# Log-sum-exp over rows: which block of rows each SBUF partition holds

## The chip, the cores and the metric

The kernel runs on one core of a Trainium2 chip. The metric is the device time of one execution in microseconds; lower is better. "The time" of a kernel is the median of several runs. A profile is one further execution, recorded by the hardware profiler, and it has a time of its own.

## The reference

The input x is 32 x 512 x 1024 in float32, 64 MiB, drawn from a normal distribution. The output is one number per row of 1024, 32 x 512 in float32.

```python
def reference(x, axis):                      # axis = -1
    x_max = np.max(x, axis=axis, keepdims=True)
    return (x_max.squeeze(axis)
            + np.log(np.sum(np.exp(x - x_max), axis=axis))).astype(np.float32)
```

The kernel computes log(sum(exp(x))) without taking the maximum away first; for values of this size that is the same number.

## The kernel before, in words

The input is seen as N = 16,384 rows of D = 1024 numbers (4 KB). P = 128 partitions share them evenly: NB = 128 rows to a partition. Rows are independent of each other, so any partition may hold any block of 128 rows, as long as the result is stored to where the rows came from. Before the change, partition p holds the rows from 128p to 128p+127, a run of 512 KB in HBM (`x_v`, and `out_v` for the result).

The work goes along the 128 rows of every partition in the 17 chunks of `CHUNKS`. A chunk is (rows, rows whose sum DVE takes, parts into which those are cut, whether DVE adds by halves). It starts with 4 rows, then 15, 16, 16, 16, 14, 13, 9, 7, 5, 4, 3, 2, and ends with four of one row. A chunk of r rows is one DMA of 128 x r x 4 KB; its source is one contiguous run of r x 4 KB for each partition, and its destination r slots of `ring`, a buffer of 51 slots of 4 KB per partition.

- Loads: `load` (L97 issues the DMA) runs on SP's queue, in the order of the chunks. Ahead of it SP waits until DVE (and ACT, L96) have used the slots that the chunk is to overwrite. The first load is moved by hand to the front of the program (`n_early`).
- Exponential: ACT waits for a chunk's semaphore (`landed[i]`) and overwrites it in place with exp, for DVE's rows in `parts` pieces (L134), then row by row for the rest, where ACT sums along the way (L161).
- Sums: DVE waits for each piece of ACT's and sums its rows into `sums`, in one instruction (L154), or for the chunks marked so row by row, adding the two halves of a row (L141).
- Logarithm: `take_logs` (L105) runs on ACT three times: over the first chunks at chunk `LN_AT`, over the following ones in the last chunk, and over the last four rows at the very end.
- Store: one DMA on ACT's queue (L173) writes `res`, 128 numbers per partition, 64 KB in all.

The order on each engine is the order in which the loop over the chunks writes its instructions; nothing is reordered by a planner. The change touches the source pattern in `load` and the target pattern of the store.

The softmax here doesn't subtract the row's maximum and nothing guards it: scores larger than these inputs give would overflow.

## Time and profile before

| | |
|---|---|
| time, median of 3 runs | 163.15 us (163.01 to 163.37) |
| the profiled execution's own time | 163.28 us |
| its span, first to last instruction | 161.4 us |
| DVE busy | 121.0 us (75%) |
| ACT busy | 115.1 us (71%) |
| read from HBM | 67.11 MB |
| SP's queue (loads) | 2448 packets |
| ACT's queue (store) | 144 packets |

How to read the profile: the span is cut into 40 equal slices, and a digit is the busy share of a slice in tenths; for DMA it is the mean over the core's 16 DMA engines. The list of DMA queues gives packets, MB, and the time in packets as a share of 16 engines' span. 2448 packets are 17 loads of 128 data packets, one per partition, and 16 that count up the semaphore, one per engine. The chain follows the work that ended last back to what released it at each step. A line of waits is: engine and line, what ended the wait, us in total, times, longest. A line of the stretches is: the stretch and its length, then for each engine busy us and instructions, the TensorE clock, the DMA's mean busy share (where packets reach over a border it can come out a little over 1) and GB/s. The trace also keeps a record of every DMA packet: its start, its duration and its bytes, without an address or an engine's number.

### The profile page before, as it was taken

What the parts mean: (1) busy time and instruction counts of PE and PEld (TensorE: products, weight loads), DVE (VectorE), ACT (ScalarE), POOL (GpSimd) and SP (SyncE); (2) the same over time, 40 slices, a digit from 0 to 9 for tenths busy, and PEclk for the clock granted to TensorE, in tenths of its full rate; (3) what the DMA queues carried; (4) which work ended last, traced back from release to release, by engine and by line L of the source; (5) the groups of instructions that cost most, each with busy time, mean ns of one, the idle gap of its engine ahead of it and who ended that gap; (6) DMA issues with size and microseconds to landing.
All of it is one profiled execution on the core that took longest, in us unless ns stands there. A gap on an engine that the chain in (4) does not pass through costs nothing.

```text
span 161.4 us, 149 instructions
## 1 busy us (share of the span) xinstructions
DVE 121.0 (75%) x46; ACT 115.1 (71%) x40; POOL 0.2 (0%) x4
## 2 busy tenths in 40 slices
DVE  0028000003999999999999699999999999999892
ACT  3170005996079960999519993999199999999995
POOL 0000000000000000000000000000000000000000
DMA  6999699989989989989979999999999999999990
GB/s 256 508 487 457 289 472 520 406 374 520 422 357 520 406 374 520 406 374 520 406 341 455 455 455 439 422 422 422 430 429 429 418 426 415 427 430 417 403 394 24
DMA packets 2592, 67.18 MB, mean 416 GB/s; under 512 B 288, under 2 KB 416, under 8 KB 928
## 3 DMA queue, kind: packets, MB, share of 16 engines
q1 hardware_dynamic: 2448, 67.11, 96.9%
q10 hardware_dynamic: 144, 0.07, 0.1%
HBM read 67.11 MB, written 0.07 MB: 416 GB/s over the span
## 4 chain that ended last, share of the span: by engine, by line
DMA 49%; DVE 29%; ACT 20%; issue 0%
DMA ring<-in_x_dram 49%; DVE sums L154 29%; ACT ring L134 17%; ACT ring L161 3%; ACT res L105 0%
## 5 line engine op out<-in xcount | busy, mean ns | idle before, releaser
L154 DVE TENSOR_REDUCE sums<-ring 128x8 f32<-128x8192 f32 (+5 forms) x14 | 111.2, 7995 | 37.3 <-ACT ring L134 37.2
L134 ACT ACTIVATE ring<-ring 128x8192 f32<-128x8192 f32 (+6 forms) x18 | 104.4, 5835 | 43.9 <-DMA ring<-in_x_dram 43.8
L141 DVE CUSTOM_DVE_ANT_0 ring<-ring 128x512 f32<-128x512 f32 x16 | 9.9, 688 | 0.0
L161 ACT ACTIVATE ring<-ring 128x1024 f32<-128x1024 f32 x9 | 9.3, 1041 | 0.0
L119 ACT ACT_TABLE_LOAD x1 | 1.3, 1283 | 0.8 <-PEq L215 0.8
L161 ACT ACTIVATION_READ_ACCUMULATOR ring<-ring 128x1 f32 x9 | 1.5, 172 | 0.0
L141 DVE DVE_READ_ACCUMULATOR2_ANT sums<- 128x1 f32 x16 | 1.3, 84 | 0.0
L105 ACT ACTIVATE res<-sums 128x81 f32<-128x81 f32 (+1 forms) x2 | 0.5, 246 | 0.0
L105 ACT ACTIVATE res<-late 128x4 f32<-128x4 f32 x1 | 0.2, 173 | 0.0
L215 POOL MEMSET const-bfloat16-1.0<- 128x1 bf16 x1 | 0.1, 103 | 0.0
L215 POOL MEMSET const-uint8-127<- 128x1 uint8 x1 | 0.1, 102 | 0.0
L215 POOL MEMSET const-float32-0.0<- 128x1 f32 x1 | 0.1, 100 | 0.2 <-issue 0.2
L215 POOL MEMSET const-float32-1.0<- 128x1 f32 x1 | 0.1, 99 | 0.0
## 6 DMA issues: line engine op xcount, KB each, us to landing
ring<-in_x_dram SPq DMA_DIRECT2D x1, 7680.0 KB, 25.2
ring<-in_x_dram SPq DMA_DIRECT2D x1, 7168.0 KB, 28.6
ring<-in_x_dram SPq DMA_DIRECT2D x1, 6656.0 KB, 35.7
ring<-in_x_dram SPq DMA_DIRECT2D x1, 4608.0 KB, 20.2
ring<-in_x_dram SPq DMA_DIRECT2D x2, 2048.0 KB, 16.1
ring<-in_x_dram SPq DMA_DIRECT2D x1, 3584.0 KB, 28.3
ring<-in_x_dram SPq DMA_DIRECT2D x1, 2560.0 KB, 27.3
ring<-in_x_dram SPq DMA_DIRECT2D x4, 512.0 KB, 27.0
```

The lines of the kernel that those rows point to most:

```text
L105: nc.scalar.activation(out=res[:, lo:hi], in_=src, func=Ln).then_inc(act_done, 1)
L119: nc.scalar.preload_act_table_set("natural_log_exp_and_others")
L134: nc.scalar.activation(out=ring[:, s + lo : s + hi], in_=ring[:, s + lo : s + hi], func=Exp).then_inc(act_done, 1)
L141: nc.vector.tensor_tensor_reduce(out=ring[:, s + j, : D // 2], in0=ring[:, s + j, : D // 2], in1=ring[:, s + j, D // 2 :], scale=1.0, scal ...
L154: nc.vector.reduce_sum(out=sums[:, row + lo : row + hi], in_=ring[:, s + lo : s + hi], axis=AX).then_inc(dve_done, 1)
L161: nc.scalar.activation(out=ring[:, s + j], in_=ring[:, s + j], func=Exp, accum_out=total(row + j),).then_inc(act_done, 1)
L215: nc = _bacc.Bacc("TRN2", target_bir_lowering=False, num_devices=1)
```

## The change

Partition p no longer holds block p of 128 rows but block p//8 + 16*(p%8): partitions 0 to 7 hold blocks 0, 16, 32, ... 112, partitions 8 to 15 blocks 1, 17, ... 113, and so on. The words that came with the change say that the 16 DMA engines then read blocks next to each other (0.5 MB apart), and that each engine's next block is 8 MB further. A helper `blocks` builds the pattern for both ends: for x with rows of D numbers and a start at row `lo`, for the output with rows of one number. In HBM a pattern has now three levels, 16 blocks at a step of 512 KB, 8 groups of them at a step of 8 MB, and the contiguous run; the SBUF side of the DMAs is as before. Nothing else changes: chunks, waits, instructions and their order are the same.

```diff
-    x_v = x_flat.rearrange("(p t) d -> p t d", p=P)
-    out_v = bass.AP(tensor=out.tensor, offset=out.offset, ap=[[NB, P], [1, NB]])
+    PER, ENG = 8, 16
+    assert P == PER * ENG
+
+    def blocks(ap, width, lo, n):
+        return bass.AP(
+            tensor=ap.tensor,
+            offset=ap.offset + lo * width,
+            ap=[[NB * width, ENG], [ENG * NB * width, PER], [1, n * width]],
+        )
...
-        nc.sync.dma_start(out=ring[:, s : s + r], in_=x_v[:, row : row + r]).then_inc(
+        nc.sync.dma_start(
+            out=ring[:, s : s + r],
+            in_=blocks(x_flat, D, row, r),
+        ).then_inc(
             landed[i], 16
         )
...
-    nc.scalar.dma_start(out=out_v, in_=res).then_inc(stored, 16)
+    nc.scalar.dma_start(
+        out=blocks(out, 1, 0, NB), in_=res
+    ).then_inc(stored, 16)
```

## The prediction

> **What bounds the kernel now.** I read the views from the whole to the part: the slices of the span, the DMA queues, the chain that ended last, the waits (engines, then SP's queue), and the stretches between stage borders.

> The slices and the queues first:

> ```profile
> span 161.4 us, 149 instructions
> ...
> DMA  6999699989989989989979999999999999999990
> ...
> q1 hardware_dynamic: 2448, 67.11, 96.9%
> q10 hardware_dynamic: 144, 0.07, 0.1%
> HBM read 67.11 MB, written 0.07 MB: 416 GB/s over the span
> ```

> The queue that carries the 17 loads has its 16 engines in packets for 96.9% of the span, 156.4 us of 161.4 us. The store's queue is 0.1%.

> The chain and the waits:

> ```profile
> DMA 49%; DVE 29%; ACT 20%; issue 0%
> ...
> ACT ring L134 <- DMA ring<-in_x_dram: 43.8, 7, 14.9
> DVE sums L154 <- ACT ring L134: 37.2, 4, 23.5
> ...
> SPq L97 <- DVE sums L154: 122.9, 7, 52.8
> ```

> The chain gives DVE and ACT half, which could mislead: a step on it is whatever released the next, and a load in flight behind another is not seen. ACT waits for nothing but loads (43.8 us), DVE only for ACT. SP's 122.9 us of waiting for free ring slots does no harm as long as the queue holds a load behind the running one. The queue's share, and this view in order of time, say it does:

> ```profile
> core 0: us, DVE busy (x) ACT busy (x) POOL busy (x), PEclk, DMA share, GB/s
> 0.00:8.00 8.00, 0.00 (x0) 1.80 (x2) 0.20 (x4) 1.00 0.95 385
> 8.00:40.00 32.00, 5.39 (x2) 16.10 (x2) 0.00 (x0) 1.00 1.02 442
> ...
> 117.00:146.00 29.00, 28.91 (x11) 29.00 (x11) 0.00 (x0) 1.00 0.99 426
> 146.00:158.00 12.00, 11.03 (x26) 11.88 (x13) 0.00 (x0) 1.00 0.94 386
> 158.00:161.40 3.40, 0.22 (x2) 1.73 (x6) 0.00 (x0) 1.00 0.07 19
> ```

> The DMA column is at 0.94 to 1.02 up to 158 us. From 117 us DVE (28.91 of 29) and ACT (29.00 of 29) are full too: the tail is packed, and all three end together. So a DMA that is uniformly slower moves the end by its whole delay, and a faster one moves the end by what it has gained up to about 84 us, where DVE waits last for a load through ACT (idle 1.59 us ahead of 91.15).

> How near is the DMA to its ceiling? The trace's packet records (start, duration, bytes; one packet per partition and load) give medians of 611 ns for 16,384 B and 2420 ns for 65,536 B. The slope, 1809 ns for 49,152 B, is 27.2 GB/s per engine and 435 GB/s for 16; what is left, some 9 ns, is a packet's fixed cost. Each engine has 156.21 us of data packets; at the median of each size it would be 155.49 us. The excess is 0.72 us per engine: 0.40 us in the first packet of twelve engines (762 to 1608 ns where the other four took 608 to 612), 0.14 us in fifteen long packets before 45 us, and 0.18 us in many of a few ns each.

> [...] The trace has no addresses; [...] the first packets start in two bunches, seven from 1.01 to 1.31 us and nine from 1.62 to 2.21. [...]

> **The change part by part.**

> *Load source patterns (17 DMAs).* Block p is still 128 rows of 4 KB, 512 KB, but partition p gets block p//8 + 16*(p%8). Bytes, contiguous runs (128 per load, 4 to 64 KB), waits and issue order do not change, so the 2448 packets stay and their time at the medians stays: 155.5 us per engine. Cost 0 in this term [...]; both bounds are below, as rivals.

> *The first packets and the scattered excess.* 0.72 us per engine can go if they come from streams that collide in HBM. [...] But twelve first packets end together with the four that started late (all ends lie between 2.19 and 2.87 us), which looks like one common first-access delay that any order has. I take 0, ends -0.72 and +0.4 (the other four slow as well).

> *Building the descriptors.* The source has one dimension more. SP takes 327 to 779 ns per issue (median 365), the engines' first packets spread over 1.2 us. Only the first load's issue is on the path; each later one has a load before it still in flight, and the cover is thinnest for small loads, whose median from issue to landing is 27.0 us for 1.3 us of own packets. Without that cover each would cost its 0.37 us. If the extra dimension doubled the first issue's 0.37 us, the end moves by 0.4; it can't gain, since 128 runs are still made. I take 0, ends 0 and +0.4.

> *The store.* It is last on ACT, 1.6 us from issue to landing, all on the path. It still has 128 runs of 512 B, of 27 ns each, 8 per engine: 0.22 us. Neighbouring partitions' runs lay side by side in 4 KB and now lie 8 KB apart. If each took twice as long: +0.22; the issue (0.373 us) doubled: +0.37. I take 0, ends -0.1 and +0.6. Nothing is queued behind it but the clearing of semaphores.

> *Compute.* Every ACT and DVE instruction keeps shape and count; rows are independent. 0. No wait is added, so nothing new stands behind one.

> Sum against the profiled execution's own time, 163.28 us (span 161.4, 1.88 around it): 0 + 0 + 0 + 0 = 163.28. That execution is 0.13 above the median of the runs, 163.15, so the forecast for a median is 163.15, say 163.1. From the ends above, the case's own range is 162.8 to 163.5. The measurement can tell about 0.2% (0.33 us) from no change.

> **The rivals.**

> *Faster: collisions in HBM go.* For: the excess hits several engines at once (four 64 KB packets near 44 us took 71 to 329 ns too long). Against: it is 0.5% at most. All of it gone gives 163.15 - 0.72 = 162.43; 0.54 of the 0.72 us lies before 45 us, so the packed tail passes it on. This includes half of it, 162.8.

> *Slower: HBM likes the new spacing less.* [...] It decides once the mean 64 KB packet is 5 ns longer (0.2%).

> *Much slower: the port match breaks.* [...] with 1.0 us ahead of the first packet, 3.4 us after the last and 1.9 around the span, 314 us. [...] 64 KB packets of 4840 ns instead of 2420, and the loads outlast every other engine at once.

> [...]

> **How the numbers follow.** Forecast (no change) 0.40; faster 0.19; slower by HBM, issue or store 0.22; much slower 0.19. Slower together 0.41. The range leaves out the port case alone (0.19) and runs from the low end of the faster case, 162.2 (0.72 us and a little of the uneven end, where engines finish between 156.9 and 158.0), to the high end of the HBM case, 168.6. The likeliest case's own range is 162.8 to 163.5.

> **What would show it.** Right: 64 KB packets stay at 2420 ns, the queue's time at 97% of the span, first packets again up to 1600 ns, ACT's wait for loads at 43.8 us, 1.6 us for the store. Faster: first packets near 611 and a queue share of 156.2 down to 155.6 us. HBM: longer packets of all sizes, evenly, and DVE's gap ahead of 91 us growing. Ports: packets doubled and DVE's share of the span near 40%. The forecast is wrong if packets change length at all, or the spread of the first starts leaves 1.2 us.

## The result, and the profile after

The changed kernel takes 327.96 us (327.31 to 329.44, 6 runs) beside 163.19 us for the kernel before (6 runs as well): 2.011 times as long, 95% interval 2.006 to 2.015. The forecast of no change is wrong, and the time lies outside its range. It is the rival named "the port match breaks", which had 314 us and a chance of 0.19; its signs came too, packets of twice the length and DVE busy for 37% of the span. "Port" is its word for a place where the writes of two engines would meet; no trace shows such a place. The profiled execution has 328.28 us, of which 326.4 are its span.

The page of the changed kernel, the lines that stand for the slices and the queues:

```profile
span 326.4 us, 149 instructions
...
DMA  8959979969989699696998799999999899999994
...
q1 hardware_dynamic: 2448, 67.11, 98.5%
q10 hardware_dynamic: 144, 0.07, 0.1%
HBM read 67.11 MB, written 0.07 MB: 206 GB/s over the span
```

The same 2448 packets and 67.11 MB, and a queue that is as busy as before (98.5% where it was 96.9%), but at half the rate. A busy DMA row therefore says that packets are in flight, not how fast their bytes flow. What changed is the duration of a packet.

Its waits, engines and SP (engine, line, what for: us in total, times, longest):

```profile
ACT ring L146 <- DMA ring<-in_x_dram: 203.7, 13, 34.3
DVE sums L166 <- ACT ring L146: 175.7, 9, 42.9
...
SPq L106 <- DVE sums L166: 243.8, 7, 76.6
```

ACT's wait for loads has gone from 43.8 to 203.7 us; DVE waits for ACT as before. SP's wait has doubled too, but it is no cause, since the queue stays full. The chain of this kernel names half of its length "another core or an unknown queue":

```profile
another core or an unknown queue 50%; ACT 32%; DMA 15%; issue 2%
```

In order of time those pieces lie between one chunk's exponentials and the next (27.48 us after the second chunk, for example), where ACT waits for the load in flight; it is the loads' share under another name.

One stretch in mid-flight (stretch and length, busy us and instructions of DVE, ACT and POOL, TensorE clock, the DMA's share, GB/s):

```profile
50.00:90.00 40.00, 16.15 (x1) 13.00 (x1) 0.00 (x0) 1.00 1.00 206
```

SP's issues of the loads (how many: min/median/max ns, first and last start):

```profile
L106 SPq DMA_DIRECT2D ring<-in_x_dram x17: 536/541/619, 0.0 to 254.0; - x17
```

The list of DMA issues has the store (KB, us to landing):

```profile
out_dram<-res ACTq DMA_DIRECT2D x1, 64.0 KB, 2.1
```

206 GB/s with the engines 100% in packets: by the packet records a 64 KB packet has a median of 5109 ns where it had 2420, and one of 16 KB 1260 where it had 611. An issue takes 541 ns at the median (365 before) and the store 2.1 us to landing (1.6 before).

The span adds up: 1.40 us to the first packet, 320.8 us from there to the end of the last load (156.9 before), 4.2 us after it, and 1.88 us around the span give 328.28.

### The profile page after: what moved, and what is told of

It is laid out like the page before. It is cut to its first block, busy times and chain, and to the rows that moved or that the text cites. A ratio compares the mean times of both kernels' runs of the same rounds, so it can differ in the third digit from the quotient of the medians.

```text
span 326.4 us, 149 instructions
## 1 busy us (share of the span) xinstructions
DVE 121.7 (37%) x46; ACT 116.0 (36%) x40; POOL 0.2 (0%) x4
## 3 DMA queue, kind: packets, MB, share of 16 engines
q1 hardware_dynamic: 2448, 67.11, 98.5%
HBM read 67.11 MB, written 0.07 MB: 206 GB/s over the span
## 4 chain that ended last, share of the span: by engine, by line
another core or an unknown queue 50%; ACT 32%; DMA 15%; issue 2%
ACT ring L146 29%; DMA ring<-in_x_dram 15%; ACT ring L173 2%; ACT res L117 0%
## 5 line engine op out<-in xcount | busy, mean ns | idle before, releaser
L146 ACT ACTIVATE ring<-ring 128x8192 f32<-128x8192 f32 (+6 forms) x18 | 104.6, 5839 | 203.7 <-DMA ring<-in_x_dram 203.7
```

The costliest lines, as they stand in the source:

```text
L146: nc.scalar.activation(out=ring[:, s + lo : s + hi], in_=ring[:, s + lo : s + hi], func=Exp).then_inc(act_done, 1)
```

## The experiments

Two theories at the start, both assumptions of mine. Ports: with the 16-long outer level of the source two engines, called a pair below, write at the same place in step and slow each other. HBM: 0.5 and 8 MB are bad distances for 16 streams. Both could give a factor of two. No trace here says which engine read or wrote what, nor whether the changed kernel's engines read blocks 0.5 MB apart, so the pairs are inferred from rates and packet lengths throughout. Where no ratio is given, the time is that of a single run, which is enough for a factor of two; the kernel before took 162.8 to 163.4 us on the same chips (single runs or medians).

### Addresses without the shape, shape without the addresses

```diff
 # e1_pad: the changed kernel, blocks 127 rows apart
-in_=blocks(x_flat, D, row, r)
+in_=bass.AP(..., ap=[[127 * D, ENG], [ENG * 127 * D, PER], [1, r * D]])     # the store is not changed
 # e2_shape: the kernel before
-in_=x_v[:, row : row + r]
+in_=bass.AP(..., ap=[[8 * NB * D, 16], [127 * D, 8], [1, r * D]])
 # e4_near: the kernel before
-in_=x_v[:, row : row + r]
+in_=bass.AP(..., ap=[[32 * D, P], [1, r * D]])
```

> The changed kernel's load pattern with its three levels (16 x 8 x run) kept, but blocks that start 127 rows apart instead of 128 (508 KB, and 7.94 MB from one group to the next), so that no pitch is a power of two. The loads then read partly the same rows twice and leave others out, so the output belongs to other rows; bytes, runs and instructions are those of the changed kernel. Ports theory [...]: nothing changes, 64 KB packets near 5110 ns, about 328 us. HBM theory [...]: packets go back to about 2420 ns and the time to about 163 us.

Measured 327.48 us, 64 KB packets at 5112 ns.

> The kernel before with its block order almost as it was (partition p starts at row 1024*(p//8) + 127*(p%8), so within 7 rows of its old place), but with a source pattern of two levels over the partitions, 16 and 8, that can't be merged into one of 128. It reads a few rows twice and leaves a few out, so the output belongs to other rows. Ports theory: the shape alone costs everything, about 327 us, 64 KB packets near 5110 ns. HBM theory: nearly the addresses of before, so about 163 us and 2420 ns.

Measured 327.89 us, 5112 ns.

> The kernel before with one level of 128 partitions as it was, but partitions that start 32 rows apart (128 KB)[...]. It reads rows several times over and covers only a part of x, so the output belongs to other rows. Ports theory: 128 partitions on both sides[...]: about 163 us, 64 KB packets 2420 ns. HBM theory: [...] well above 163 us.

Measured 163.09 us, 2418 ns. The page of the second of these three, with the addresses of before and the shape of after:

```profile
span 326.0 us, 149 instructions
...
q1 hardware_dynamic: 2448, 67.11, 98.3%
```

The three together leave little for HBM: small distances between the partitions' starts in the old shape are fast (128 KB, 2418 ns), almost the old addresses in the new shape are slow (5112 ns), and distances that are no powers of two change nothing (5112 ns as well). What e4_near lacks, a far jump from one partition's block to the next one's (8 MB in the changed kernel), the 32 x 4 kernel below has (16 MB), and it is fast.

### Other outer lengths

```diff
-    PER, ENG = 8, 16
+    PER, ENG = 4, 32       # e3_32x4
+    PER, ENG = 2, 64       # e5_64x2
+    PER, ENG = 16, 8       # e9_8x16
```

The question is whether an outer level of 32 behaves like one of 128 or like one of 16.

> The changed kernel with 32 x 4 in place of 16 x 8: partition p holds block p//4 + 32*(p%4), right output. [...] about 163 us, 64 KB packets 2420 ns. [...] about 328 us and 5110 ns. HBM theory: [...] no faster than 328 us. I expect 328 at 60 in 100.

Measured 163.56 us, ratio 1.0023 (1.0008 to 1.0037). Its page:

```profile
span 161.6 us, 149 instructions
...
q1 hardware_dynamic: 2448, 67.11, 96.9%
```

Its issues on SP:

```profile
L106 SPq DMA_DIRECT2D ring<-in_x_dram x17: 534/550/619, 0.0 to 130.4; - x17
```

So a source with three levels is not slow as such. My expectation (328 us at 60 in 100) was wrong: fast packets are not tied to an outer length of 128.

> The changed kernel with 64 x 2 in place of 16 x 8 (partition p holds block p//2 + 64*(p%2), output right). The 32 x 4 pattern ran at the speed of one of 128[...]. [...] about 163.5 us and 2420 ns. If 32 was a special case[...]: about 328 us and 5110 ns.

Measured 164.92 us, 64 KB packets at 2418 ns at the median, so on the fast side, as expected. Its 60 KB packets had a mean of 2340 ns (median 2267); I have not followed that.

> The changed kernel with 8 x 16 in place of 16 x 8 (partition p holds block p//16 + 8*(p%16), output right): 8 engines [...]. Ports theory: 64 KB packets near 5110 ns as in the changed kernel, on half the engines: 67.11 MB at some 103 GB/s, 650 us, and the kernel about 657 us. If [...] packets are slow only when 16 of them are at work: 2420 ns, 308 us, and the kernel about 315 us.

Measured 603.97 us. Stretches of it, in the large loads and in the last ones:

```profile
100.00:450.00 350.00, 82.07 (x9) 62.78 (x11) 0.00 (x0) 1.00 0.50 107
560.00:600.00 40.00, 9.13 (x19) 17.29 (x18) 0.00 (x0) 1.00 0.46 154
```

Half the engines (share 0.50; the queue has 2312 packets, 17 x 8 fewer than with sixteen), and 64 KB packets at 5074 ns: an outer level of 8 is as slow per packet as one of 16. Most of the miss from 657 us lies behind the 64 KB loads: those ended at 331.9 us, where twice the changed kernel's time would be 342, and the rest took 266 us for 302. 4 KB packets had 159 ns there, their full speed (a median of 161 in the kernel before), and 12 KB packets anything from 460 to 926 ns (461 before). Why small packets were fast again was not shown.

### The same rate from four engines and from eight

```diff
 # the kernel before, each load in n DMAs of w partitions
-nc.sync.dma_start(out=ring[:, s : s + r], in_=x_v[:, row : row + r])
+for q in range(n):     # e8_quarters: n 4, outer 8, inner 4; e12_four: 4, 4, 8; e13_eight: 2, 8, 8
+    nc.sync.dma_start(out=ring[w * q : w * q + w, s : s + r], in_=bass.AP(...,
+        ap=[[NB * D, outer], [outer * NB * D, inner], [1, r * D]]))
 ...                    # ACT waits for 16 * n in place of 16
```

> The kernel before with every load cut into four DMAs of 32 partitions, whose source has the levels 8 x 4 x run (blocks in a new order, the store not changed with it, so the output belongs to other rows). An outer level of 8 leaves 8 engines[...]. Ports theory: 64 KB packets at 2420 ns though the source has three levels; 8 engines carry 218 GB/s, so 67.11 MB take 308 us and the kernel about 315 us. If a three-level source makes packets slow by itself: 5110 ns, and about 655 us.

Measured 318.51 us, 64 KB packets at 2418 ns. The 218 GB/s expected are eight times the 27.2 GB/s of the prediction's slope; a stretch has 216:

```profile
40.00:280.00 240.00, 108.15 (x26) 93.25 (x20) 0.00 (x0) 1.00 0.50 216
```

> The kernel before with each load cut into four DMAs of 32 partitions whose source has the levels 4 x 8 x run (blocks in a new order, the store not changed with it, so the output belongs to other rows). Four engines[...]. Ports theory [...]: 64 KB packets at 2420 ns, 109 GB/s, 616 us and the kernel about 622 us. [...] 5100 ns, and about 1300 us.

Measured 628.18 us, 2418 ns.

> The same with two DMAs of 64 partitions and the levels 8 x 8 x run (output again of other rows): eight engines with runs of eight[...]. Ports theory: 64 KB packets near 5100 ns, 103 GB/s, about 650 us. If eight engines leave room: 2420 ns, 308 us, kernel about 315 us.

Measured 596.69 us, 5094 ns at the median (4 KB packets at 159 ns again). A stretch of the kernel with four engines:

```profile
50.00:550.00 500.00, 108.14 (x26) 93.26 (x20) 0.00 (x0) 1.00 0.25 108
```

And one of the kernel with eight:

```profile
95.00:185.00 90.00, 17.96 (x2) 21.87 (x3) 0.00 (x0) 1.00 0.51 108
```

Twice the engines (0.51 of 16 where it was 0.25) carry the same 108 GB/s (105 and 106 in other stretches), where the eight engines of the first kernel carry 216 from blocks that lie just as close (0.5 MB). The inner level of eight is the same in the last two. So neither three levels, nor eight engines (both in the first kernel, 2418 ns), nor an inner level of eight (in the second, 2418 ns) is slow by itself; what is left, as I read it, is engines that meet in pairs.

### Parting the partners

If two engines are slow because they go through the same places at the same time, it may be enough that one of them is some packets behind. An extra DMA on a few engines does that; with 256 KB on each it is as long as four of their 64 KB packets.

```diff
+        if i == 2:                       # ahead of the third load
+            nc.sync.dma_start(out=ring[: 8 * k, 35:43], in_=bass.AP(..., offset=x_flat.offset,
+                ap=[[NB * D, k], [16 * NB * D, 8], [1, 8 * D]])).then_inc(held, 16)
+        if i == 3:
+            nc.sync.wait_ge(held, 16)
```

On e13_eight: k = 4 (e14_eight_lag), 2 (e16_eight_lag2), 3 (e17_eight_lag3). On the changed kernel: k = 4 (e7_lag), 2 (e11_lag2), one engine with 17 runs of 16 KB (e10_lag1), and k = 12, 8 and 4 one after the other ahead of the second load (e15_all_apart). The runs with four, two and one lagging engine among sixteen were made first, and the expectations of the others refer to them; they are told after the two runs that were to part every pair. How many engines carry an extra DMA is in the traces: each has one packet of 4 B more for every such engine. Which engines these are is not in the traces; that each of them parts one pair is an assumption.

> The run with eight engines, plus one DMA of 4 x 8 runs of 32 KB ahead of the third load, which four engines carry and SP waits for ahead of the fourth load. [...] Ports theory: 64 KB packets of the third load at 2420 ns, and of later loads as long as the lag lasts; kernel well under the run without the lag. If a lag never helps (as with one, two and four lagging among 16 engines): near 5100 ns throughout, and the time of the run without the lag or a few us more.

Measured 393.72 us: the 1 MB more to carry takes 203 us off. Three stretches of the kernel with eight engines and no lag:

```profile
20.00:90.00 70.00, 4.42 (x1) 3.62 (x1) 0.00 (x0) 1.00 0.50 105
95.00:185.00 90.00, 17.96 (x2) 21.87 (x3) 0.00 (x0) 1.00 0.51 108
185.00:300.00 115.00, 32.75 (x4) 19.03 (x3) 0.00 (x0) 1.00 0.50 106
```

The same three with the lag, which comes with the third load, near 92 us:

```profile
20.00:90.00 70.00, 4.42 (x1) 3.62 (x1) 0.00 (x0) 1.00 0.50 105
95.00:185.00 90.00, 33.43 (x3) 26.95 (x3) 0.00 (x0) 1.00 0.49 204
185.00:300.00 115.00, 51.50 (x7) 48.54 (x10) 0.00 (x0) 1.00 0.50 216
```

The same share, the same number of engines, the same load addresses: 105 GB/s until the lag comes, 204 and 216 after it. Of the third load 107 of 128 packets were within a tenth of full speed, and all 256 of the fourth and fifth took between 2418 and 2428 ns. It did not last to the end: from the tenth load on there were slow packets again.

> The changed kernel plus three DMAs between the first and the second load, carried by 12, 8 and 4 engines, 256 KB on each; SP waits for them ahead of the fourth load, whose slots they use. Output as the reference's. [...] If slow pairs held back the engines[...] in the runs with one, two and four lagging engines: now most packets of the second to fourth load are near full speed (2267 ns for 60 KB, 2420 for 64 KB), until waits for ring slots bring the engines together again. If ports are not the place: near 5100 ns throughout, and about 328 us plus some 20 to 30 for the 6 MB more.

Measured 318.69 us, 9 us under the changed kernel with 6.3 MB more. Stretches with the lags and after all sixteen had started a load together again:

```profile
76.00:106.00 30.00, 2.37 (x1) 13.00 (x1) 0.00 (x0) 1.00 0.93 390
125.00:316.00 191.00, 95.71 (x44) 83.65 (x35) 0.00 (x0) 1.00 0.96 210
```

In the fourth load 116 of 128 packets were fast. SP then waited for ring slots: at 110 us only 8 engines had a packet in flight, at 120 us only 4, and at 121 us all sixteen began the fifth load together. In the fifth to the twelfth load none was fast.

> The changed kernel with one more DMA on SP's queue between the second and the third load: 4 x 8 runs of 32 KB into ring slots that are still free, whose source has an outer level of 4, so that only four engines carry it (1 MB, 256 KB each); SP waits for it before the fourth load, which overwrites those slots. The output is the reference's. Ports theory [...]: the four engines fall four packets behind their partners, these four pairs no longer meet, and in the third and fourth load half of the 64 KB packets take about 2420 ns and the other half still about 5110; the end stays near 328 us, since the other four pairs still meet and set it. A theory in which the three-level pattern makes each packet slow by itself, or in which HBM is short: all packets stay near 5110 ns, and the extra 1 MB adds some 5 us.

Measured 335.55 us, 64 KB packets at 5092 ns, none fast: against the ports theory as I had stated it.

> As before with the extra DMA's outer level at 2: two engines carry 256 KB each, 8 runs of 32 KB. Output as the reference's. Ports theory: if the two are partners, nothing changes (all near 5100 ns); if they are not, both pairs come apart, and 4 of 16 engines have packets near 2420 ns in the following loads. If no pairs exist: all near 5100 ns here and in the run with one lagging engine too.

Measured 336.88 us, 5102 ns, none fast.

> As the run with the lagging four engines, in which no packet became fast, but the extra DMA has 17 runs of 16 KB to 17 partitions, and [...] a single engine carries all 272 KB and falls some two to four 64 KB packets behind. Output as the reference's. A single engine can't take its partner along. Ports theory: it and its partner no longer meet all the time, so in the third to seventh load 2 of 16 engines have packets well under 5000 ns, down to 2420, and 14 stay near 5100; the end stays near 330 us. If the slow packets do not come from two engines that meet in step (four lagging engines that change nothing speak for that): all packets stay near 5100 ns but for a few while the extra DMA runs. The ports theory explains the run with four only if those four were two whole pairs.

Measured 339.38 us, 5105 ns, none fast. But the one engine's own packets say where they met others. In order of time (start us, ns):

```
48.7 1232   50.0 1191   51.1 1314   52.4 1308   53.7 1291   55.0 1288   56.3 1313   57.6 1314
58.9 1335   60.2 1795   62.0 1865   63.8 1861   65.7 1531   67.2 1306   68.5 1313   70.0 1208   71.0 1259
```

Three of them, the tenth to the twelfth, take about three times 611 ns, and just two 64 KB packets of other engines are long in that time: 6706 ns from 58.8 us and 6980 ns from 59.5 us, where the rest have 5170 to 5190. I read those three as a meeting. Yet its other fourteen packets were slow too (1191 to 1531 ns), where the theory had left it room. From this I took it that pairs which still meet hold back the others.

> The run with eight engines and a lag, with the extra DMA on two engines instead of four (output again of other rows): two of the four pairs come apart, two still meet. If pairs that meet hold back those that are apart (the reading of the runs with one, two and four lagging among sixteen): nearly all 64 KB packets of the third load stay near 5100 ns, and the kernel stays near the 597 us of eight engines without a lag. If each pair is on its own: half of the packets of the third load at 2420 ns.

Measured 545.24 us; packets of the third load between 3822 and 5099 ns, none at full speed. They grow shorter from load to load (medians of 4772, 4598 and 4349 ns in the third to fifth). The stretch after the lag:

```profile
95.00:185.00 90.00, 16.15 (x1) 13.00 (x1) 0.00 (x0) 1.00 0.51 116
```

> The same with the extra DMA on three engines: three of four pairs come apart, one still meets. Held back by one pair: packets stay near 5100 ns and the time near 597 us. Each pair on its own: three quarters of the packets of the third load at 2420 ns.

Measured 575.80 us, and the same stretch:

```profile
95.00:185.00 90.00, 18.26 (x2) 22.17 (x3) 0.00 (x0) 1.00 0.50 181
```

In the third load 97 of 128 packets were fast (three of four pairs, each on its own, would give 96), in the fourth 110, in the fifth 72, in the sixth 96, in the seventh none (counted in order of start). From there on it is slower than the run with two lagging engines, and it ends 31 us behind it. So the theory that a pair still meeting holds back all others has fallen too: one of four does not, at least for four loads. Two of four do (none of 128 packets fast), and so did four, six and seven of eight, if each of the four, two or one lagging engines among sixteen parts one pair. What makes that difference is open, and so is the place where engines meet. What the runs settle is that eight engines at the same load addresses are slow without a lag (105 GB/s) and fast with four of them behind (204 and 216).

### The store, and what the order is worth

```diff
 # e6_store: the kernel before
-nc.scalar.dma_start(out=out_v, in_=res)
+nc.scalar.dma_start(out=blocks(out, 1, 0, NB), in_=res)     # 16 x 8, as in the changed kernel
 # e4_timed: e4_near again, in 21 runs
```

> The kernel before with only the store's target in the levels 16 x 8 (its numbers go to rows of other partitions, so the output is in another order). The store in the changed kernel took 2.1 us from issue to landing instead of 1.6, and its issue 0.614 us instead of 0.373. It is last on the path: about +0.3 to +0.5 us, 163.5 to 163.7, ratio 1.002 to 1.003. If the store doesn't care: 1.000.

Measured 163.52 beside 163.03 us, ratio 1.0029 (1.0017 to 1.0040): about +0.5 us, at the top of what was expected; its issue took 0.628 us, its landing 2.1.

> The kernel with 128 partitions in one level, starting 128 KB apart, timed[...]. It reads only a part of x, several times over, so the output belongs to other rows. This is what reading blocks next to each other is worth when nothing else changes. No gain from order: 163.2 us, ratio 1.000. All of the scattered excess gone: down to 162.5, ratio 0.996. One look gave 163.09 beside 163.35.

Measured 162.82 beside 163.03 us, ratio 0.9992 (0.9983 to 1.0002): no difference that can be told. Its stretch in the large loads:

```profile
40.00:85.00 45.00, 45.00 (x5) 29.39 (x5) 0.00 (x0) 1.00 1.00 433
```

Starts 128 KB apart in place of 512 KB are worth at most 0.2%. The 32 x 4 order, whose packets stay fast, is slower by about what a store in three levels costs (1.0023 beside 1.0029). No version here beats the kernel before.

## Why the prediction was wrong, point by point

- *What bounds the kernel.* Right: the loads did, and a uniform change of packets went to the end in full.
- *"Cost 0 in this term."* This step failed: the term of the load source patterns was put at 0, and the loads took 320.8 us from the first packet to the end of the last load where they had taken 156.9, nearly all of the 164.8 us that were lost. That a 16 x 8 source is carried like one of 128 partitions was an assumption of mine that no trace of before showed, and it held the other case at 0.19. The runs showed that the source's outer level decides, with the same 128 partitions as the destination: 32, 64 and 128 have 64 KB packets of 2418 to 2420 ns, 16 has 5109 and 8 has 5074. What each engine is given in these cases was not shown.
- *The ports rival.* Right in its signs, its price too low: a packet was taken at 4840 ns (twice 2420) and has 5109. Over the loads that is 320.8 us for 308, which is 67.11 MB at half of the 435 GB/s of the slope; the other terms were 1.40 us for 1.0, 4.2 for 3.4, and 1.88 for 1.9. Against that half, some 218 GB/s, stand 67.11 MB / 320.8 us = 209 GB/s. The two prices also disagreed with each other: packets of twice the length would have been 2 x 155.5 = 311 us, not 308. And the rival has no place for what the lags showed: with four, two or one of sixteen engines behind the others, no 64 KB packet was fast (5092, 5102 and 5105 ns).
- *The HBM rival.* Wrong in this case: the addresses moved the time by nothing that can be told. Only the runs with shape and addresses apart tell the two theories from each other. The loss that set this rival's upper end was an estimate that no trace of before showed.
- *Faster by fewer collisions.* Nothing that can be told: 0.9992 (0.9983 to 1.0002) for starts 128 KB apart in the old shape. The first sixteen packets end as close together in the changed kernel (2.35 to 2.93 us) as before.
- *Descriptors.* I took 0 of 0 to +0.4 us. The median issue went from 365 to 541 ns, and the first packet came 0.39 us later (1.40 us for 1.01). That need not have moved the end: the first packets of the sixteen engines start at 1.61 us on average where they started at 1.55, and in the 32 x 4 kernel, whose issues are as long, the last load ended at 157.7 us where it had ended at 158.0. So 0 may have been right.
- *The store.* I took 0 of -0.1 to +0.6; it is about +0.5 us. With the loads left fast, this alone would have brought 163.15 to about 163.6, just outside the range of the forecast case (163.5).
- *A packet's fixed cost.* The slope of 1809 ns for 49,152 B leaves 611 - 603 = 8 ns, not 9; nothing rests on it.
- *The range.* It left out the case that came, because that case was held at 0.19. What the profile could not decide, how the engines share a source of 16 x 8, should have had even odds.

## What to carry to other kernels

## What the runs showed of the hardware that I had not expected

- Adding work made a kernel a third faster: 1 MB on four of eight engines, 596.69 to 393.72 us, with the same addresses and the same number of engines; what the extra work changed, as I read it, is their phase (105 GB/s before it, 204 and 216 after it).
- A slow packet takes a little more than twice a fast one: 5109 ns for 2 x 2420. In each of the changed kernel's three loads of 64 KB packets the first sixteen packets to start and the fifth sixteen are shorter than the rest (4933 to 4971 ns in the first of them, where the others have 5086 to 5128).
- How many engines lag matters in a way that pairs alone do not explain: with three of eight behind, 97 of 128 packets of the first load were fast, with two of eight none. Why is open.
- A pattern of three levels costs SP some 180 ns more per issue, whether its packets are then fast (550 ns at the median) or slow (541), where two levels take 365.
